# A hybrid decoder trunk: the delta-net stage with TensorE's work in program order, its head parts woven at set distances, and convolutions in thirds

## The chip, the cores and the metric

One core of a Trainium2 chip runs the whole program once. The metric is the device time of that core in microseconds (us), the median of several runs. TensorE multiplies matrices (PE in the profile, PEld its weight loads), VectorE (DVE), ScalarE (ACT) and GpSimd (POOL) work element by element, SyncE (SP) issues most DMAs. Each engine works through its own instructions in a fixed order, and waits on the others by semaphores.

## The reference

A sequence of 1,024 tokens and 16 learned meta tokens (T = 1,040 rows of 1,024) goes through one block with three branches: gated delta-net attention (8 heads of 128), Mamba-2 SSD, and sliding-window attention. They are merged, projected, and followed by an MLP. The change lies in the first branch:

```python
qkv = jax.nn.silu(causal_dwconv(jnp.concatenate([q, k, v], axis=-1), conv_w))   # 4 taps
q, k = l2norm(q), l2norm(k)
beta = jax.nn.sigmoid(b)
g = -jnp.exp(a_log) * jax.nn.softplus(a + dt_bias)          # log decay
...
decay = jnp.exp(jnp.where(tri_incl, gam[..., :, None] - gam[..., None, :], -jnp.inf))
a_low = jnp.where(tri_strict, einsum("bhncd,bhnsd->bhncs", kb, k) * decay, 0.0)
sol = triangular_solve(a_low + eye, rhs, left_side=True, lower=True, unit_diagonal=True)
...
def step(s_state, inp):                                     # over chunks, in order
    v_new = u_c - w_c @ s_state
    o_c = qd_c @ s_state + a_c @ v_new
    s_state = s_state * exp(gl_c) + kt_c.T @ v_new
...
o = rmsnorm(o, norm_w) * jax.nn.silu(gate)
```

## The kernel before

All products are float32 or float32 split in two parts: an operand is a high part (h) plus a low rest (l), and a projection is three products (high by high, high by low, low by high) over 8 blocks of 128 input rows: 24 matmuls for each chunk of columns. The normed input lies in SBUF as `hnh` and `hnl`; the weight's rest is computed by GpSimd (`split_w`, line 118).

A convolution (`conv_steps`, line 342) is a projection over chunks of 348, 346 and 346 columns, 72 matmuls; ScalarE copies each chunk out (`raw`), and when all three are there VectorE does one multiply and three multiply-adds over all 1,040 columns (line 358), then the silu in two halves by a tanh on ScalarE (line 360) and one VectorE step (line 361). A gate (`gdn_gate`, named gg) is a projection over two chunks of 512.

For each head, `gdn_kr` (line 399 on) transposes k (ktp), takes its norms, builds the decay masks dm and the decayed factor qt from rows fetched by DMA (gm), and forms the 128x128 blocks w of the system from k times k (kk; kk0 for the 32 rows of the meta chunk). `gdn_solve` (line 494) inverts the diagonal blocks of 32: it sends them through DRAM into one layout for all (lbd to lb), does 31 pairs of VectorE steps xt and ub (lines 513 and 515), sends the result back through DRAM (ubd to w), and transposes three blocks on VectorE (tt, line 527). `gdn_vr` transposes and scales v (vtp, vt), `gdn_qr` forms q times k (kq, then dm by VectorE, line 478), transposes q for its norms (qtp) and multiplies qt by q on GpSimd (line 469).

What then follows for the head before is its tail. `gdn_levels` (line 532) composes blocks of 32 to 64 and 128 by small matmuls lq, lu, lt, each with a copy by ScalarE. `gdn_scan` (line 576) runs over nine chunks: ks (k times state S), rr on VectorE (line 590), py (line 596), its copy y on ScalarE (line 598), psn (line 603), the new S on VectorE (line 608), and the outputs po. Each step waits for the one before. `gdn_final` normalises: f (VectorE, then a power on GpSimd), vt times f, transposes yf, product with the gate.

The order of the work: `stage_gdn` (line 643) writes head by head: v convolution, final of the head before the last, kr, gate of the last head (with its tail woven in), solve, vr, q convolution, k convolution of the next head, the rest of the tail, qr. Weaving is a generator: a tail yields a number of columns (`WL, WR, WY, WS = 1800, 3200, 2000, 2200`), and each matmul of a projection takes its width off that number (`tick`); at zero the tail makes its next step. So steps of the tail stand between matmuls of a projection. But this order is only written: a scheduler then orders the instructions of each engine by its own estimate of when each is ready, and by priority. Small products outside the weave, such as kk and ktp, are placed by it.

The numbers that follow the names in the listings (`k_3534`) are buffers. "Chain 3" is the levels and the scan of head 3. Heads are counted from 0; the k and v convolutions of head 0 run before the stage, beside the projection smm of the small inputs (b, a, dt), whose transposes (smt), cumulative sums (smg) and rows (smr) make the decays.

## Time and profile before

| | us |
|---|---|
| median of three runs | 2673.28 (2671.59 to 2673.66) |
| profiled execution, its own time | 2672.7 |
| its span | 2670.7 |
| TensorE busy in the span | 2540.5 |
| VectorE busy | 1606.1 |
| ScalarE busy | 1034.6 |
| GpSimd busy | 621.5 |
| mean granted clock of TensorE | 0.979 of full |

The delta-net stage takes from about 78 to 726 us, the SSD stage follows to about 1,140, then sliding window, merge, output projection and MLP. A row of the timeline has start, duration, engine, line, operation, output and inputs, and a count where several of one kind follow each other; in brackets how long the engine had idled and for whom. A row of the waits has the waiting instruction, the one waited for, the total, how often, and the longest. A row of the groups has total busy time and the mean in ns. "Granted clock" is the share of full speed that TensorE was given.

### The profile page before, as it was taken

What the parts mean: (1) busy time and instruction counts of PE and PEld (TensorE: products, weight loads), DVE (VectorE), ACT (ScalarE), POOL (GpSimd) and SP (SyncE); (2) the same over time, 40 slices, a digit from 0 to 9 for tenths busy, and PEclk for the clock granted to TensorE, in tenths of its full rate; (3) what the DMA queues carried; (4) which work ended last, traced back from release to release, by engine and by line L of the source; (5) the groups of instructions that cost most, each with busy time, mean ns of one, the idle gap of its engine ahead of it and who ended that gap; (6) DMA issues with size and microseconds to landing.
All of it is one profiled execution on the core that took longest, in us unless ns stands there. A gap on an engine that the chain in (4) does not pass through costs nothing.

```text
span 2670.7 us, 37466 instructions
## 1 busy us (share of the span) xinstructions
PE 2540.5 (95%) x13983; PEld 2171.0 (81%) x13983; DVE 1606.1 (60%) x3039; ACT 1034.6 (39%) x2581; POOL 621.5 (23%) x491
## 2 busy tenths in 40 slices
PE   6999899999999999999999999999999999999998
PEld 5888788888889989878887888888877788878886
DVE  5776677667557656567673012232426877686878
ACT  4334344334423313355553122121246454444443
POOL 3222222222223323321221222222241000041230
PEclk9989899999999999999999999999999999999999
DMA  3211111111111122231213122131334544566422
GB/s 116 74 37 54 53 53 53 46 48 45 60 63 56 64 72 71 61 83 49 69 52 119 48 67 91 48 111 48 114 122 153 194 169 151 206 243 201 143 87 98
DMA packets 123124, 246.65 MB, mean 92 GB/s; under 512 B 39766, under 2 KB 40182, under 8 KB 122942
## 3 DMA queue, kind: packets, MB, share of 16 engines
q1 hardware_dynamic: 117390, 231.76, 25.9%
q0 software_dynamic: 4544, 11.14, 1.7%
q8 instruction: 110, 1.80, 0.3%
q10 hardware_dynamic: 1008, 1.34, 0.1%
q14 instruction: 72, 0.59, 0.1%
HBM read 183.76 MB, written 54.01 MB: 89 GB/s over the span
## 4 chain that ended last, share of the span: by engine, by line
PE 72%; DVE 18%; issue 3%; DMA 3%; ACT 2%; POOL 2%; SPq 0%; DVEq 0%; POOLq 0%; ACTq 0%
PE dn L1409 10%; PE mgm L149 10%; PE pr L1064 9%; PE up L1214 8%; PE pso L1116 3%; PE x L149 3%; PE gg L149 2%; PE aq L149 2%; DVE xt L513 2%; PE q L149 2%; PE z L149 2%; PE v L149 2%; PE b L149 2%; DVE ub L515 2%; PE c L149 2%
## 5 line engine op out<-in xcount | busy, mean ns | idle before, releaser
L1409 PE MATMUL dn<-wh,ah 128*128 128x512 f32 x448 | 175.4, 391 | 4.3 <-ACT wh L1154 4.3
L1409 PE MATMUL dn<-wl,ah 128*128 128x512 f32 x448 | 175.7, 392 | 0.9 <-POOL wl L1155 0.9
L1409 PE MATMUL dn<-wh,al 128*128 128x512 f32 x448 | 175.5, 392 | 0.0
L1064 PE MATMUL pr<-yl,wph 128*128 128x512 f32 x384 | 150.3, 391 | 1.9 <-DVE yl L137 1.9
L1064 PE MATMUL pr<-yh,wph 128*128 128x512 f32 x384 | 150.2, 391 | 1.9 <-ACT wph L123 1.0
L1064 PE MATMUL pr<-yh,wpl 128*128 128x512 f32 x384 | 149.5, 389 | 0.0
L1074 DVE SCALAR_TENSOR_TENSOR gt<-gt,pr 128x512 f32<-128x512 f32 x32 | 21.9, 687 | 197.5 <-PE pr L1064 197.5
L1155 DVE TENSOR_TENSOR al<-ar,ah 128x512 fp32r<-128x512 f32 x112 | 98.7, 884 | 43.1 <-ACT ah L1154 42.8
L1155 POOL TENSOR_TENSOR wl<-wd,wh 128x512 fp32r<-128x512 f32 x48 | 71.9, 1503 | 194.2 <-ACT wh L1154 63.6
L125 POOL TENSOR_TENSOR wpl<-wpr,wph 128x1024 fp32r<-128x1024 f32 x24 | 61.2, 2549 | 228.0 <-ACT wph L123 217.4
L1154 ACT ACTIVATE ah<-ar 128x512 fp32r<-128x512 f32 x112 | 70.3, 628 | 108.5 <-PE dn L1409 82.8
L123 ACT ACTIVATE wph<-wpr 128x1024 fp32r<-128x1024 f32 x24 | 25.5, 1061 | 210.8 <-PE pr L1064 184.1
L1409 PEld LDWEIGHTS dn<-wh,ah 128*128 128x128 f32 x448 | 84.8, 189 | 22.6 <-ACT wh L1154 4.8
L1409 PEld LDWEIGHTS dn<-wl,ah 128*128 128x128 f32 x448 | 84.8, 189 | 18.9 <-POOL wl L1155 1.2
L149 PE MATMUL mgm<-hnh,mgl 128*128 128x512 f32 x384 | 99.5, 396 | 0.0
L149 PE MATMUL mgm<-hnh,mgh 128*128 128x512 f32 x384 | 99.3, 396 | 0.0
L1409 PEld LDWEIGHTS dn<-wh,al 128*128 128x128 f32 x448 | 84.8, 189 | 17.5
L149 PE MATMUL mgm<-hnl,mgh 128*128 128x512 f32 x384 | 99.0, 396 | 0.0
L125 POOL TENSOR_TENSOR mgl<-mgr,mgh 128x1024 fp32r<-128x1024 f32 x24 | 57.6, 2401 | 164.6 <-PE mgm L149 149.1
L1064 PEld LDWEIGHTS pr<-yl,wph 128*128 128x128 f32 x384 | 72.1, 188 | 19.3 <-DVE yl L137 4.5
L1064 PEld LDWEIGHTS pr<-yh,wph 128*128 128x128 f32 x384 | 72.1, 188 | 19.3 <-ACT yh L136 2.8
L149 PEld LDWEIGHTS mgm<-hnh,mgh 128*128 128x128 f32 x384 | 71.8, 188 | 16.3
(479 smaller groups left out, 7075.6 us busy)
## 6 DMA issues: line engine op xcount, KB each, us to landing
ar<-acd SPq DMA_DIRECT2D x106, 256.0 KB
wu<-in_wup SPq DMA_DIRECT2D x37, 512.0 KB
acd<-s SPq DMA_DIRECT2D x64, 256.0 KB
mgr<-in_win SPq DMA_DIRECT2D x24, 512.0 KB
wpr<-in_wpr SPq DMA_DIRECT2D x24, 512.0 KB
yr<-yd SPq DMA_DIRECT2D x48, 256.0 KB
acd<-c SPq DMA_DIRECT2D x48, 256.0 KB
dms<-rowd SPq DMA_DIRECT2D x16, 512.0 KB
```

Of the source, the lines that this page charges most:

```text
L123: nc.scalar.activation(wh, wr, AF.Copy)
L125: nc.gpsimd.tensor_tensor(wl, wr, wh.bitcast(F32), op=ALU.subtract)
L149: nc.tensor.matmul(ps[:, 0:n], a[:, k, :], b[k][:, c0:c0 + n], start=(i == 0 and k == 0), stop=(i == 2 and k == KT - 1))
L513: nc.vector.tensor_tensor(tv, lb[:, j:j + 1, j + 1:32].broadcast_to([3 * n_, n, m]), ub[:, 0:n, j:j + 1].broadcast_to([3 * n_, n, m]), op= ...
L515: nc.vector.tensor_tensor(ub[:, 0:n, j + 1:32], ub[:, 0:n, j + 1:32], tv, op=ALU.add)
L1064: nc.tensor.matmul(ps, x[:, k, :], y, start=(k == 0 and j == 0), stop=(k == KT - 1 and j == 2))
L1074: nc.vector.scalar_tensor_tensor(t, t, 1.0, ps, op0=ALU.add, op1=ALU.mult)
L1116: nc.tensor.matmul(ps, x[k, th][:, ts], y, start=(k == 0 and j == 0), stop=(k == KT - 1 and j == 2))
L1154: nc.scalar.activation(hi, src, AF.Copy)
L1155: (eng or nc.vector).tensor_tensor(lo, src, hi.bitcast(F32), op=ALU.subtract)
L1214: self.nc.tensor.matmul(ps, x[:, k * P:(k + 1) * P], ops[k][y], start=(j == 0 and k == 0), stop=(j == 2 and k == 3))
L1409: nc.tensor.matmul(acc[t], x[:, t * P:(t + 1) * P], y, start=(i == 0 and m == 0), stop=(i == n - 1 and m == 2))
```

## The change

- During the delta-net stage every matmul and transpose keeps its place in the written order on TensorE (`pin`, `keep_in_program_order`). The other engines' instructions are still placed by the scheduler.
- Several generators run at once, each with its own remaining distance and a scale for it. Not only the tail is woven, but also kr, vr, qr and final, with distances of their own; the tail of head 0 starts 41,000 columns after it is entered, with its distances times 0.55, the others at 7,000, the last at 24,000 with 0.55.
- Convolutions of the stage run in thirds (`conv_pieces`): ScalarE copies a chunk out twice, once scaled by the last tap, VectorE does three multiply-adds, the silu follows for that chunk.
- GpSimd's weight rest and qt times q are four instructions each instead of one. Its product kt times ktc goes; ScalarE scales py by ktc instead (ys), beside the copy y.
- rr, S, w, dm, vt, the transposes tt, the copies of levels, y, ys and po have high priority. The tt transposes are the first step of the tail, no longer the last of the solve; the solve is called at the end of kr.
- At the end of the stage the b and c convolutions of the SSD stage's first group are issued in `stage_gdn`, with the last tail still woven in, and then the last final.

The diff, cut to its core:

```diff
-WL, WR, WY, WS = 1800, 3200, 2000, 2200
+WL, WR, WY, WS = 1800, 3800, 2400, 2900
+RK, RW, RQ = 1500, 3000, 4500
...
-        nc.gpsimd.tensor_tensor(wl, wr, wh.bitcast(F32), op=ALU.subtract)
+        n = 2 if self.pin else KT
+        for k in range(0, KT, n):
+            nc.gpsimd.tensor_tensor(wl[:, k:k + n, :], wr[:, k:k + n, :], wh[:, k:k + n, :].bitcast(F32), op=ALU.subtract)
...
+    def mm(self, *a, **k):
+        i = self.nc.tensor.matmul(*a, **k)
+        return self.tc.keep_in_program_order(i) if self.pin else i
...
     def tick(self, n):
...
+        for co in list(self.cos):
+            co[1] -= n
+            if co[1] <= 0:
+                self.step(co)
...
+    def conv_pieces(self, wt, tag, wcol, name):
...
+        for c0, n, ps in self.proj(wt, CH_ALL, name):
+            d = dst[:, c0:c0 + n]
+            nc.scalar.activation(raw[:, 3 + c0:3 + c0 + n], ps, AF.Copy)
+            nc.scalar.activation(d, ps, AF.Copy, scale=w(3))
+            for j in range(3):
+                nc.vector.scalar_tensor_tensor(d, raw[:, c0 + j:c0 + j + n], w(j), d, op0=ALU.mult, op1=ALU.add)
+            th = self.bt("th", name + "th", [P, 528])[:, 0:n]
+            nc.scalar.activation(th, d, AF.Tanh, scale=0.5)
+            nc.vector.scalar_tensor_tensor(d, th, 1.0, d, op0=ALU.add, op1=ALU.mult)
+            yield
...
-        nc.gpsimd.tensor_tensor(kt, kt, ktc.unsqueeze(2).broadcast_to([P, NC, P]), op=ALU.mult)
-        st.update(qt=qt, dm=dm, w=w, w0=w0, kt=kt, vsc=vsc, bk=bk)
+        st.update(w=w, w0=w0, kt=kt, vsc=vsc, bk=bk, ktc=ktc)
+        self.gdn_solve(st)
...
-            nc.scalar.copy(y[0:n], ps[0:n, 0:P])
+            ys = self.sm.tile([P, P], F32, name="ys", bufs=1)
+            with self.tc.high_priority():
+                if c < NC - 1:
+                    nc.scalar.activation(ys[0:n], ps[0:n, 0:P], AF.Copy, scale=s["ktc"][0:n, c:c + 1])
+                if c > 0:
+                    nc.scalar.copy(y[0:n], ps[0:n, 0:P])
...
     def stage_gdn(self, cur):
         prev = old = None
+        self.pin = True
         for h in range(GH):
...
+                if old:
+                    self.weave(self.gdn_final(old))
+                self.weave(self.gdn_kr(cur), 14000)
+                tail = self.weave(self.gdn_tail(prev), 41000 if h == 1 else 7000, 0.55 if h == 1 else 1.0)
+                self.gdn_v(cur)
+                self.weave(self.gdn_vr(cur), 14000)
+                self.gdn_gate(prev)
+            self.gdn_q(cur)
+            self.weave(self.gdn_qr(cur), 14000)
+            nxt = self.gdn_k(h + 1) if h < GH - 1 else None
             if prev:
+                self.drain(tail)
             old, prev, cur = prev, cur, nxt
+        self.weave(self.gdn_final(old))
+        tail = self.weave(self.gdn_tail(prev), 24000, 0.55)
         self.gdn_gate(prev)
+        self.pin = False
+        st = dict(g=0)
+        self.ssd_b(st)
+        self.ssd_c(st)
         self.drain()
...
     def gdn_tail(self, s):
+        self.gdn_trans(s)
+        yield 4000
         yield from self.gdn_levels(s)
```

Three places show what moves. The first is TensorE at the start of the stage, where smt, smg and smr make the decays of all heads and q is the convolution of head 0. Before:

```order
L256 MATMUL smt<-ident,su 128x32 x6
L149 MATMUL q<-hnh,qh 128x348 x2
L256 MATMUL smt<-ident,su 128x32 x3
L149 MATMUL q<-hnh,qh 128x348 x6
...
L149 MATMUL q<-hnh,ql 128x346 x6
L292 MATMUL smg<-val,tri 128x288
L303 MATMUL smr<-tri,val 32x128 x9
```

Now:

```order
L162 MATMUL smt<-ident,su 128x32 x9
L158 MATMUL smg<-val,tri 128x288
L158 MATMUL smr<-tri,val 32x128 x9
L158 MATMUL q<-hnh,qh 128x348
L162 MATMUL ktp<-ident,k_323 128x128 x4
L158 MATMUL q<-hnh,qh 128x348 x5
```

All of q's matmuls stand behind smg and smr now; 68 of its 72 stood between the last smt and smg before.

The second is where the levels of chain 0 begin on TensorE. Before, they were in the v convolution of head 2, behind the q convolution of head 1 and the k convolution of head 2:

```order
L475 MATMUL kq<-q_1653,k_1025 128x128 x8
L149 MATMUL v<-hnh,vh 128x348 x4
L485 MATMUL qtp<-ident,q_1653 128x128 x4
L149 MATMUL v<-hnh,vh 128x348 x4
L149 MATMUL v<-hnl,vh 128x348 x3
L544 MATMUL lq<-tt,w 32x32 x8
```

Now they are in the gate of head 0, ahead of the q convolution of head 1:

```order
L162 MATMUL vtp<-ident,v_1180 128x128
L158 MATMUL gg<-hnh,ggh 128x512
L158 MATMUL gg<-hnl,ggh 128x512 x2
...
L158 MATMUL gg<-hnl,ggh 128x512 x3
L158 MATMUL lq<-tt,w 32x32 x16
L158 MATMUL gg<-hnl,ggh 128x512 x2
L158 MATMUL lu<-w,qs 32x32 x16
L158 MATMUL gg<-hnl,ggh 128x512
L158 MATMUL gg<-hnh,ggl 128x512
L158 MATMUL lt<-qs,w 32x32 x8
```

They moved ahead by two convolutions, and stand one or two gate matmuls apart.

The third is VectorE at the end of the solve in one of the middle heads. Before (ub ends the solve; k is the convolution of the next head):

```order
L515 TENSOR_TENSOR ub<-ub,xt 99x11
L590 SCALAR_TENSOR_TENSOR rr<-ks,neg,vt 128x128
L608 SCALAR_TENSOR_TENSOR S<-S,egl,psn 128x128
L590 SCALAR_TENSOR_TENSOR rr<-ks,neg,vt 128x128
L353 TENSOR_SCALAR k_3534<-kraw,cols 128x1040
L358 SCALAR_TENSOR_TENSOR k_3534<-kraw,cols,k_3534 128x1040
L478 SCALAR_TENSOR_TENSOR dm<-kq,bk,dm 128x128
L358 SCALAR_TENSOR_TENSOR k_3534<-kraw,cols,k_3534 128x1040
L527 STREAM_TRANSPOSE tt<-w 32x8x32 x2
```

Now:

```order
L574 TENSOR_TENSOR ub<-ub,xt 99x11
L681 SCALAR_TENSOR_TENSOR S<-S,egl,psn 128x128
L657 SCALAR_TENSOR_TENSOR rr<-ks,neg,vt 128x128
L535 SCALAR_TENSOR_TENSOR dm<-kq,bk,dm 128x128 x8
L681 SCALAR_TENSOR_TENSOR S<-S,egl,psn 128x128
L590 STREAM_TRANSPOSE tt<-w 32x8x32 x3
L657 SCALAR_TENSOR_TENSOR rr<-ks,neg,vt 128x128
L394 SCALAR_TENSOR_TENSOR k_4662<-kraw,cols,k_4662 128x348
```

The last rr of the scan stands behind the tt transposes now, all eight dm ahead of them, and the steps of the k convolution behind both.

278 lines of the change are left out of this document (159 added, 119 removed).

## The prediction

> **What bounds the kernel now.** I read the page's slices first, then the busy time by stretch, then the waits of TensorE, and last the timeline at each long wait. The slices say which engine to follow:
>
> ```profile
> PE   6999899999999999999999999999999999999998
> PEclk9989899999999999999999999999999999999999
> ```
>
> TensorE is at nine tenths or more nearly everywhere; past the start and ahead of the last slice the only eights, slice 5 of its busy row and slices 3 and 5 of its granted clock (66.8 us a slice), lie in the delta-net stage (about 78 to 726 us), the only stage whose order the change touches. The busy time by stretch (us; TensorE, its loads, VectorE, ScalarE, GpSimd; clock; DMA), cut where the convolutions of v of heads 3, 4 and 7 and the first one of the next stage begin:
>
> ```profile
> core 0: us, PE busy (x) PEld busy (x) DVE busy (x) ACT busy (x) POOL busy (x), PEclk, DMA share, GB/s
> 77.90:279.40 201.50, 184.39 (x1260) 166.13 (x1259) 143.74 (x354) 81.52 (x265) 54.33 (x38) 0.94 0.19 54
> 279.40:364.00 84.60, 78.78 (x528) 70.65 (x527) 57.61 (x157) 32.91 (x109) 21.26 (x15) 0.88 0.17 45
> 364.00:598.90 234.90, 216.25 (x1580) 195.99 (x1579) 165.56 (x397) 98.70 (x326) 60.16 (x44) 0.99 0.18 53
> 598.90:726.40 127.50, 118.37 (x868) 103.55 (x867) 76.20 (x177) 54.28 (x189) 28.37 (x22) 0.97 0.16 53
> ```
>
> TensorE idles 648.5 - 597.8 = 50.7 us in the stage, and part of its busy time runs at a low clock. The third row is three even heads, 78.3 us each with 6.2 idle. What it waits for (total, times, longest):
>
> ```profile
> PE py L596 <- DVE rr L590: 20.7, 10, 2.6
> PE qtp L485 <- DVE dm L478: 11.8, 6, 2.9
> PE yf L638 <- DVE vt L632: 5.2, 3, 2.2
> PE lq L544 <- DVE tt L527: 3.3, 2, 3.1
> PE kk L445 <- DVE w L442: 3.2, 1, 3.2
> ```
>
> All are waits for VectorE, an engine that is busy two thirds of the time: small steps of the scan (rr) and of the masks (dm) stand in its queue behind convolution steps and blocked ones. The sizes, from VectorE's groups in one solve (total, mean ns, idle before):
>
> ```profile
> L358 DVE SCALAR_TENSOR_TENSOR q<-qraw,cols,q 128x1040 f32<-128x1040 f32 x3 | 3.9, 1292 | 0.0
> L590 DVE SCALAR_TENSOR_TENSOR rr<-ks,neg,vt 128x128 f32<-128x128 f32 x5 | 1.7, 344 | 0.5 <-PE ks L588 0.5
> ```
> Two blocks, from the timelines of VectorE and GpSimd (start, duration):
>
> ```profile
> 496.96 0.24 DVE L513 TENSOR_TENSOR xt<-lb,ub 99x77 f32<-99x77 f32 x1
> 497.64 2.37 DVE L513 TENSOR_TENSOR xt<-lb,ub 99x80 f32<-99x80 f32 x1
> 507.96 2.22 DVE L513 TENSOR_TENSOR xt<-lb,ub 99x40 f32<-99x40 f32 x1
> ...
> 497.53 2.39 POOL L125 TENSOR_TENSOR vl<-vr,vh 128x1024 fp32r<-128x1024 f32 x1 [14.17 <-ACT sqo L617]
> ...
> 507.75 2.37 POOL L469 TENSOR_TENSOR qt<-qt,q 128x1024 f32<-128x1024 f32 x1 [1.70 <-DVE q L361]
> ```
>
> A multiply of 0.24 us takes 2.37 when a whole-tile GpSimd operation began just ahead of it, and ends with it. The low clock has its places too:
>
> ```profile
> 304.86 0.69 PE L544 MATMUL lq<-tt,w 32*32 32x32 f32 x16 [3.08 <-DVE tt L527]
> ...
> 182.00:188.00 6.00, 6.00 (x36) 4.98 (x35) 1.30 (x6) 2.48 (x9) 0.00 (x0) 0.50 0.01 3
> 188.00:194.00 6.00, 6.00 (x23) 5.40 (x22) 2.23 (x9) 0.73 (x2) 0.00 (x0) 0.50 0.00 0
> ...
> 309.00:317.00 8.00, 8.00 (x52) 5.88 (x52) 0.00 (x0) 1.34 (x4) 0.00 (x0) 0.50 0.25 64
> ```
>
> After the levels of chains 0 and 2, TensorE is busy without a gap at half clock for 12 us and more; half of 12 is 6 us lost each time.
>
> **The change, part by part.** The profiled execution spans 2670.7 us and took 2672.7 itself, 0.6 under the median of 2673.28; I sum against 2672.7. About 0.2%, 5.3 us, is what a measurement of this kernel can tell from no change. TensorE's work is the same in kind and number, so only its waits, its clock and the end of the stage count.
>
> Stretch one, 77.9 to 279.4, has two edits that cost. First, q of head 0 no longer stands between the small transposes (smt) and the cumulative sums (smg); VectorE's chain for the gates lies between them:
>
> ```profile
> 77.99 0.46 DVE L264 TENSOR_TENSOR v<-smt,par 128x288 f32<-128x288 f32 x1 [0.79 <-PE smt L256]
> ...
> 80.27 1.95 DVE L272 RECIPROCAL den<-den 128x288 f32<-128x288 f32 x1
> ...
> 83.59 3.91 DVE L280 SCALAR_TENSOR_TENSOR p<-p,s 128x288 f32<-128x288 f32 x8
> ...
> 88.52 0.46 DVE L288 TENSOR_TENSOR val<-spl,fac 128x288 f32<-128x288 f32 x1
> ```
>
> From 77.9 to 89.0 TensorE has nothing: +11.1 us. The cover was q, and nothing else is placed there. At half clock afterwards I add 1.7.
>
> Second, the levels of chain 0 stand before q of head 1, inside the gate of head 0; before, they came two convolutions later. Will their data be there? The first v convolution started at 107.98:
>
> ```profile
> 107.98 1.44 PE L149 MATMUL v<-hnh,vh 128*128 128x348 f32 x8
> ...
> L513 DVE TENSOR_TENSOR xt<-lb,ub 99x84 f32<-99x84 f32 (+23 forms) x31 | 11.1, 357 | 0.8
> L515 DVE TENSOR_TENSOR ub<-ub,xt 99x84 f32<-99x84 f32 (+23 forms) x31 | 6.9, 224 | 0.9
> ...
> 295.47 0.18 DVE L515 TENSOR_TENSOR ub<-ub,xt 99x11 f32<-99x11 f32 x1
> ...
> 304.38 0.43 DVE L527 STREAM_TRANSPOSE tt<-w 32x256 f32<-32x256 f32 x1 [0.49 <-DMA w<-ubd]
> ```
>
> It now starts 12.8 us later, and 3.6 more for the transposes and products placed ahead of it: 124.4. A third of the convolution and its first steps lie before the solve of head 0: about 129.7. The two groups of 31 are a solve of an even head (484.2 to 511.9); xt's mean holds the two blocks, so I take ub's: 62 steps at 0.224 us are 13.9 us; with the other VectorE work that the new order puts between them (nine convolution steps, w, vt, one gate half: some 11 us) and a block or two it ends near 155.5. The round through memory from the last step to the first transpose is 304.38 - 295.65 = 8.7: data at 164. TensorE is there at 124.4 + 11.4 (convolution) + 3.1 + 8.6 (37 gate matmuls) + 1.0 = 148.5. So it waits 16 us (8 if VectorE's order gives way, 21 if GpSimd still blocks it). These levels are close together again, as at 304.86 and longer after a wait; the clock costs between 1.7 and 7, and I take 4.
>
> The Trainium skill's page "TensorE: Matmul & The Clock Gate", Part 1, says that an idle window of some 3.4 us halves the clock and some 3.4 us of work restores it. By that this wait would cost 1.7 us of clock and the sum would be 2.3 lower; the 12 us at 0.50 with TensorE busy don't agree with so quick a return.
>
> What goes in this stretch: its busy time at the even heads' clock is 184.39 x 0.94 / 0.98 = 176.9, and the 17.1 us of waits. What is left per head I take as 2.5 us: rr, S, dm and the copies now go first in VectorE's and ScalarE's queues, and a convolution step is a third as long (1.29 to 0.43), so rr's 2.6 and dm's 2.9 should fall under 1; but the transposes tt now stand ahead of the last chunk's rr, and wait for the 8.7 us round of the solve. Between the solve's end and tt VectorE's new order has only one chunk's steps and eight dm, some 5 us of TensorE's time by the chunk rows below; so rr waits 4 us where the solve ends as late as its place, 0 where it ends early: I take 2. The copies that ScalarE has more of, beside other work, add 0.5. Stretch one: 176.9 + 11.1 + 1.7 + 16 + 4 + 2 x 2.5 = 214.7, against 201.5: +13.2.
>
> Stretch two had a low clock and two stalls: 78.78 x 0.88 / 0.98 = 70.7, and 2.5: 73.2 against 84.6: -11.4. Stretch three: 216.25 + 3 x 2.5 = 223.75 against 234.9: -11.15.
>
> Stretch four: the last chunks of chain 6 are run off before the last gate with nothing between them. What a chunk then takes shows in its three steps of before:
>
> ```profile
> 194.69 0.38 PE L588 MATMUL ks<-S,k 128*128 128x128 f32 x2
> ...
> 195.54 0.47 PE L596 MATMUL py<-rr,w 128*128 128x128 f32 x2
> ...
> 196.42 0.49 PE L603 MATMUL psn<-y,kt 128*128 128x128 f32 x2
> ...
> 197.35 0.49 PE L588 MATMUL ks<-S,k 128*128 128x128 f32 x2
> ```
>
> A chunk is 2.66 us from ks to ks, about 1.1 of it its own matmuls; three without cover lose near 5 us, and 2 for the clock. With 3 more for the yf transposes and the levels of chain 7 (yf waited 5.2 in all before) it is 118.4 + 10 = 128.4 against 127.5: +0.9. (0 to 7 more if the levels of chain 7, dense at a scale of 0.55, halve the clock.)
>
> The rest costs nothing or little. GpSimd loses kt times ktc and ScalarE gains eight copies and the scaled convolution copies, three for each of three convolutions a head:
>
> ```profile
> L598 ACT COPY y<-py 128x128 f32<-128x128 f32 (+1 forms) x9 | 2.4, 263 | 12.7 <-PE py L596 12.6
> L349 ACT ACTIVATE kraw<-k 128x346 f32<-128x346 f32 (+1 forms) x3 | 1.4, 461 | 5.0 <-PE k L149 5.0
> ...
> 442.20:519.80 77.60, 71.05 (x529) 64.37 (x528) 55.01 (x133) 32.90 (x109) 19.91 (x15) 1.00 0.18 53
> ```
>
> 8 x 0.26 + 9 x 0.46 = 6.2, so ScalarE goes from 32.9 busy of 77.6 to about 39, beside TensorE; were its cover gone, a copy of a level would be 1 to 3 us late. Quarters cut the longest block from 2.4 to 0.6. The first b and c convolutions only moved in the code. Sum: 13.2 - 11.4 - 11.15 + 0.9 = -8.5; 2672.7 - 8.5 = 2664.2 us.
>
> **The rivals.**
>
> *Faster still: the start hides itself, and the even heads get near their floor.* If solve 0 is done when its levels come (less of VectorE's other work before it), 16 + 4 go; if a head keeps 1.5 us of waits, six heads give 6 more: 2664 - 26 = 2638. For it: the rr waits have causes that the change removes. Against it: the reckoning of 164 against 148.5.
>
> *Slower: the last chunk waits for tt in every head.* If the solve isn't shortened by the quarters, its data come 4 us late or more: rr of the last chunk stands behind tt in VectorE's queue, py behind rr, po and the following k matmuls behind py. At 7 us a head instead of 2.5 the six heads give back 27: 2691. It decides from 2.5 + 8.5 / 6 = 3.9 us a head upwards; from 4.8 it is slower by more than the bound. For it: before, tt stood after that rr; twelve quarters now start about a solve, and each can catch a step for up to 0.6 (a quarter of 2.4), 7.2 us in all where the blocks of 497.64 and 507.96 cost 4.1 over a free step. The page "SBUF — State Buffer" of the Trainium skill, section "Who interferes with whom", has a VectorE instruction with two SBUF inputs and a GpSimd one that reads SBUF hold the shared pair for the whole instruction, whoever is first; by that rule the quarters shorten the longest block and not their total, which the two blocks above agree with and no run here shows for quarters. Against it: VectorE is free for 77.6 - 55.0 = 22.6 us of an even head, so a late solve can catch up.
>
> *The change does nothing on balance*: the start costs 28 and the even heads bring 28, so 2673, within 5.
>
> **How the numbers follow.** My forecast 0.32 (0.26 of it faster by over 0.2%, 0.06 within). The faster rival 0.26, the slower 0.28, no balance 0.14 (0.08 within, 0.06 slower). Faster 0.52, same 0.14, slower 0.34. The likeliest case alone runs from 2652 (wait of 8, clock of 1.7) to 2676 (wait of 21, clock of 7). Together the range goes from 2628, somewhat under the faster rival, to 2692, the slower one.
>
> **What would show it.** Right: the smg wait of 11 us near 78 to 89 and a wait for tt of 8 to 21 us ahead of the first lq; the v convolution of head 3 starting later than 279.4 by 10 to 16, and then heads of 73 to 75 us; rr and dm waits of under 1 us; no xt step over 1 us. Wrong: q filling the time to smg; levels of chain 0 without a wait; heads of 78 us or more with py waiting for the last rr, which would be the slower rival; heads of 71, the faster one. The stages after the delta net should keep their length.

## The result and the profile after

| | before | after |
|---|---|---|
| median, us | 2672.44 (2668.52 to 2673.66, 4 runs) | 2718.61 (2716.36 to 2719.69, 4 runs) |
| profiled span, us | 2670.7 | 2718.0 |

The ratio is 1.0174 [1.0157, 1.0192]: the kernel got slower by 46 us; faster was forecast, and the time lies above the predicted range of 2628 to 2692. The slices of the page say at once that the loss isn't spread evenly (TensorE's busy tenths and its granted clock, 68 us a slice):

```profile
PE   6679889888999999999999999999999999999998
PEclk8879999999999999999999999999999999999999
```

The stage lies in slices 2 to 12 (77.9 to 768.6 us). Cut at the same instructions as in the prediction (v convolutions of heads 3, 4 and 7, first x convolution), and with that x convolution as a fifth row:

```profile
77.90:309.60 231.70, 187.59 (x1263) 168.91 (x1264) 147.74 (x429) 94.91 (x312) 54.17 (x72) 0.87 0.16 46
309.60:391.70 82.10, 72.78 (x529) 65.81 (x528) 55.71 (x152) 38.52 (x129) 21.76 (x29) 0.98 0.17 50
391.70:637.60 245.90, 218.02 (x1581) 197.19 (x1580) 166.87 (x451) 115.34 (x382) 64.78 (x85) 0.98 0.17 50
637.60:768.60 131.00, 117.58 (x846) 103.28 (x846) 71.89 (x178) 57.74 (x193) 28.06 (x32) 0.95 0.14 43
768.60:799.40 30.80, 28.42 (x188) 27.21 (x187) 21.20 (x20) 12.62 (x31) 8.37 (x6) 1.00 0.20 69
```

| stretch | before | after | difference | forecast |
|---|---|---|---|---|
| one, to v of head 3 | 201.5 | 231.7 | +30.2 | +13.2 |
| two, head 3 to 4 | 84.6 | 82.1 | -2.5 | -11.4 |
| three, heads 4 to 7 | 234.9 | 245.9 | +11.0 | -11.15 |
| four, to x | 127.5 | 131.0 | +3.5 | +0.9 |
| x convolution on | the rest | the rest | +5 | 0 |

The sum is +47, as the spans say. Every middle head now takes 82.0 us (473.7 to 555.7 and its neighbours), where 74 was forecast. The waits of TensorE (total, times, longest), over the stage:

```profile
PE yf L162 <- DVE vt L707: 24.4, 7, 4.2
PE ks L158 <- DVE S L681: 15.9, 12, 2.8
PE lq L158 <- DVE tt L590: 13.5, 2, 12.4
PE smg L158 <- DVE val L304: 11.2, 1, 11.2
PE vtp L162 <- DVE vt L510: 10.3, 1, 10.3
PE py L158 <- DVE rr L657: 7.2, 10, 1.2
PE lq L158 <- ACT qs L608: 4.0, 6, 1.7
```

The waits for rr and dm have shrunk as forecast: py waits 7.2 in all instead of 20.7, and the 11.8 of qtp are gone. But the list is longer than before at the top. Three waits belong to the start (smg, vtp, lq for tt); yf and ks recur in every head.

**The start.** The wait of smg is the forecast one, 11.2. That of vtp (transposes of v of head 0) was overlooked. The timeline of ScalarE, GpSimd and VectorE shows its chain:

```profile
95.69 0.27 ACT L457 COPY kt<-ktp 128x128 f32<-128x128 f32 x1 [0.32 <-PE ktp L162]
...
99.06 1.05 ACT L439 ACTIVATE qt<-gm 128x1024 f32<-128x1024 f32 x1
...
101.64 0.29 ACT L460 ACTIVATE jk<-kt 128x128 f32<-128x128 f32 x1
...
106.97 1.80 POOL L473 TENSOR_TENSOR vsc<-vs,ppos 128x9 f32<-128x9 f32 x1 [1.95 <-DVE vs L471]
...
108.81 1.55 DVE L510 TENSOR_TENSOR vt<-vtp,vsc 128x512 f32<-128x512 f32 x3 [1.74 <-POOL vsc L473]
...
109.55 0.47 PE L162 MATMUL vtp<-ident,v 128*128 128x128 f32 x1 [10.32 <-DVE vt L510]
```

The norms of k (jk) could begin at 95.7, when the last kt is copied, but ScalarE takes them from 101.6 on, in turn with the exponentials of dm, which wait for the rows gm by DMA. From the norms come the factors vsc, from them vt, and two groups of four transposes fill the buffers; the ninth transpose, first of the third group, waits for the first vt, and the rest of the q convolution waits behind it, in order. Then the first lq of chain 0 in TensorE's timeline:

```profile
173.72 1.06 PE L158 MATMUL lq<-tt,w 32*32 32x32 f32 x16 [12.41 <-DVE tt L590]
```

and the slices of 8 us behind it (columns as in the prediction: five busy times, clock, DMA):

```profile
174.00:182.00 8.00, 6.51 (x75) 4.84 (x73) 7.06 (x28) 2.15 (x5) 0.00 (x0) 0.50 0.01 2
182.00:190.00 8.00, 8.00 (x51) 6.20 (x50) 1.78 (x8) 1.89 (x4) 0.00 (x0) 0.50 0.00 1
190.00:198.00 8.00, 8.00 (x45) 6.65 (x45) 6.39 (x23) 2.76 (x9) 2.79 (x4) 0.87 0.24 66
```

A wait of 12.4 (16 was forecast), and half clock until about 192, 18 us after work began again. Some 17 us of that were busy, so 8 to 9 us were lost (4 was forecast).

**A middle head.** 82.0 us hold 72.7 busy and 9.3 idle, of which 4.1 are yf's wait and 2.3 those of ks. In the timelines of VectorE, ScalarE, GpSimd and TensorE the chain of yf reads (the last row is a group of VectorE over the head, with total and mean):

```profile
472.25 0.98 ACT L392 ACTIVATE k<-k,cols 128x348 f32<-128x348 f32 x2
...
472.57 3.65 POOL L128 TENSOR_TENSOR ggl<-ggr,ggh 128x256 fp32r<-128x256 f32 x4 [4.66 <-PE k L158]
...
472.89 6.01 DVE L394 SCALAR_TENSOR_TENSOR k<-kraw,cols,k 128x348 f32<-128x348 f32 x7 [0.87 <-ACT k L392]
...
478.82 0.15 DVE L704 SCALAR_TENSOR_TENSOR f<-ms,qe 128x8 f32<-128x8 f32 x1
...
481.04 1.23 DVE L707 TENSOR_TENSOR vt<-vt,f 128x1024 f32<-128x1024 f32 x1 [0.17 <-POOL f L706]
...
482.32 1.11 PE L162 MATMUL yf<-ident,vt 128*128 128x128 f32 x4 [4.14 <-DVE vt L707]
...
L394 DVE SCALAR_TENSOR_TENSOR q<-qraw,cols,q 128x346 f32<-128x346 f32 (+1 forms) x9 | 5.1, 570 | 0.0
```

The last ks of the scan (471.25) is the last reader of one of two k buffers, and the first step of the new k convolution writes into it: ScalarE's scaled copy. Though its raw copy was made at 459.2, the scaled one comes at 472.25. All of k's steps then land together on VectorE. Seven of them take 6.01 us: the first five 0.78 to 1.41 each, beside GpSimd's work, the other two 0.57, which is also what a step of q takes (570 ns in the mean). The final's f stands behind all seven, and yf, held in its place, waits. So a step of a third takes 0.57, and not the 0.43 (a third of 1.29) of the prediction. What makes ks wait for S in every head was not tried apart.

### The profile page after: what moved, and what is told of

Same layout as the page of the kernel before. It is cut to its first block, busy times and chain, and to the rows that moved or that the text cites. A ratio compares the mean times of both kernels' runs of the same rounds, so it can differ in the third digit from the quotient of the medians.

```text
span 2718.0 us, 37896 instructions
## 1 busy us (share of the span) xinstructions
PE 2539.1 (93%) x13983; PEld 2169.6 (80%) x13983; DVE 1612.6 (59%) x3171; ACT 1077.9 (40%) x2725; POOL 635.8 (23%) x597
## 4 chain that ended last, share of the span: by engine, by line
PE 70%; DVE 18%; ACT 4%; issue 3%; DMA 2%; POOL 2%; SPq 0%; DVEq 0%; ACTq 0%; POOLq 0%
PE dn L158 10%; PE mgm L158 9%; PE pr L158 9%; PE up L158 9%; PE gg L158 3%; PE pso L158 3%; PE aq L158 3%; PE pv L158 2%; PE x L158 2%; DVE ub L574 2%; DVE xt L572 2%; PE z L158 2%; PE c L158 2%; PE b L158 2%; PE v L158 1%
## 5 line engine op out<-in xcount | busy, mean ns | idle before, releaser
L128 POOL TENSOR_TENSOR mgl<-mgr,mgh 128x1024 fp32r<-128x1024 f32 x24 | 57.6, 2400 | 167.0 <-PE mgm L158 150.8
```

The costliest lines, as they stand in the source:

```text
L128: nc.gpsimd.tensor_tensor(wl[:, k:k + n, :], wr[:, k:k + n, :], wh[:, k:k + n, :].bitcast(F32), op=ALU.subtract)
```

## The experiments

The theory at the outset: with the order held, each wait of TensorE adds to the time, so taking away the cause of one shortens every head by it. The rivals: the clock, or another engine's queue, takes it back; or the quarters on GpSimd cost more than they bring. A head is the distance from one v convolution's first matmul to the next.

| kernel | edit | v of head 3 at | middle heads | x at | median us |
|---|---|---|---|---|---|
| before | | 279.4 | 77.6 to 84.7 | 726.4 | 2672.4 |
| after | | 309.6 | 82.0 | 768.6 | 2718.6 |
| e1 | final later | | 81.9 | | 2724.2 |
| e2 | order free | 288.7 | 82.0 to 84.9 | | 2700.3 |
| e5 | third k buffer | 307.2 | 81.3 to 82.8 | 765.7 | 2720.6 |
| e7 | whole convolutions | 313.1 | 85.4 to 86.3 | 790.5 | 2740.0 |
| e9 | scan ends earlier | 309.5 | 76.0 to 83.8 | 753.9 | 2705.8 |
| e17 | halves apart | 309.0 | 82.0 to 89.7 | 786.1 | 2736.5 |
| e13 | halves apart, scan earlier | 308.6 | 73.9 | 730.3 | 2687.9 |
| e19 | e13, head 0 free | 308.6 | 73.9 | 726.8 | 2680.1 |
| e14 | e13, order free | 288.2 | 73.9 | 703.0 | 2658.8 |
| e18 | e14, third k buffer | 285.5 | 73.8 to 74.6 | 699.7 | 2654.5 |

### Does taking a wait away shorten a head?

First the final is moved back, behind VectorE's burst of k steps:

```diff
 def gdn_final(self, s):
-        yield 8000
+        yield 19500
```

> The changed kernel with one number changed: the transposes yf of the final come 19,500 columns after the final's first step, not 8,000. Nothing else. Theory 1 (waits at the woven places add up: yf's wait is a wait of its own, because f stands behind seven convolution steps and a power on GpSimd, and v's first chunk of 24 matmuls is all that covers it): the yf waits, 24.4 us in seven places, go to under 4, the even head falls from 82.0 to 78.0 +- 0.7 us and the kernel by 20 to 25 us, to about 2695. Theory 2 (the heads are bound by a chain through VectorE and ScalarE, and TensorE's waits only move): the levels, kk or the scan wait instead, the head stays at 81 us or more and the kernel at 2713 or more.

2724.24 us, ratio to before 1.0201 [1.0136, 1.0266]. yf's wait fell from 24.4 to 1.2 us in all, and the heads stayed at 81.9. The longest wait but those of the start, then one head and a slice of 4 us in a later one:

```profile
PE lq L158 <- ACT qs L608: 17.6, 6, 4.4
```

```profile
394.10:476.00 81.90, 74.99 (x528) 67.37 (x528) 55.48 (x151) 38.58 (x128) 21.76 (x29) 0.94 0.17 50
...
570.00:574.00 4.00, 3.55 (x38) 3.10 (x38) 0.28 (x1) 0.95 (x3) 0.00 (x0) 0.50 0.00 0
```

The levels, now without yf's wait ahead of them, come into the burst: the second half of lq waits for a copy in ScalarE's queue, and the clock halves. Against the changed kernel's head, idle time fell from 9.3 to 6.9, and busy time rose from 72.7 to 75.0. The theory that waits add up falls. Next the cause itself goes: a third buffer for k (paid for by one buffer of the tanh, and by a constant that is loaded by DMA instead of copied by GpSimd).

```diff
-        self.tags = dict(raw=2, th=3, qv=1, gm=1, k2=2, kt=3, vt=2, dm=2, w=2, gt=1, qt=2)
-        self.xtags = dict(lb=1, ub=1, xt=1, qs=1, x4=2, hs=3, vb=2)
+        self.tags = dict(raw=2, th=2, qv=1, gm=1, k2=2, kt=3, vt=2, dm=2, w=2, gt=1, qt=2)
+        self.xtags = dict(k2b=1, lb=1, ub=1, xt=1, qs=1, x4=2, hs=3, vb=2)
...
-        return dict(h=h, k2=self.together(self.gdn_in(h, 1, "k2", "k"))[0])
+        return dict(h=h, k2=self.together(self.gdn_in(h, 1, "k2b" if h % 3 == 2 else "k2", "k"))[0])
```

> The changed kernel with a third buffer for the convolved k (the tanh pieces have two buffers instead of three for it, and the identity of the solve is loaded by a DMA instead of copied by GpSimd, to make room). Theory 3: a third of the k convolution writes its scaled copy straight into the destination, and that buffer is still read by ks of the chain two heads back until its last chunk; so ScalarE's scaled copies stand until 472.25 though the first raw copy is there at 459.23, and all nine VectorE steps of k burst into the next head. With a third buffer the steps of two thirds of k come ahead of tt, VectorE's 5 us of idle time there are used, and the even head falls from 82.0 to 75 to 78 us, the kernel by 25 to 40 us to 2680 to 2695. Theory 2b (the head is bound by the sum of VectorE's work with its blocks, not by this buffer): heads of 81 us or more, the kernel over 2710.

2720.55 us, ratio 1.0198 [1.0116, 1.028]. yf's wait halved (11.7 in all, none over 1.8), so the buffer was a cause of it; heads 81.3 to 82.8 with 73.9 to 75.5 busy at clocks of 0.94 to 0.96. Both edits together:

> The same with yf 19,500 columns after the final's first step, as in the first experiment, where it gained nothing. Theory 3: there ScalarE's queue stood behind the tanh of k, which waited for the burst, and the wait moved from yf to lq; with the burst gone the later yf gains what is left of its wait: 0 to 2 us a head below the third buffer alone, and lq waits for qs under 1 us each. Theory 2b: as there, heads of 81 us or more.

2728.71 us, ratio 1.0229, heads of 82.4 to 86.9 and lq waiting 21.1 us for qs. The wait was removed or halved in three ways, and the median rose by 2 to 10 us: what a head gains in waits it loses in clock. The next edit ends the tail earlier, all its distances shortened:

```diff
-    tail = self.weave(self.gdn_tail(prev), 41000 if h == 1 else 7000, 0.55 if h == 1 else 1.0)
+    tail = self.weave(self.gdn_tail(prev), 41000 if h == 1 else 7000, 0.55 if h == 1 else 0.8)
```

> The changed kernel with the distances of every middle tail at 0.8: the last ks of a chain comes some 7 us earlier in the k convolution, and so the buffer of k is free earlier; no buffer is added. Theory 3: the burst of k's steps starts earlier by as much, yf's wait of 4.1 us falls under 1, the head to 77 to 79 us, the kernel to 2690 to 2705. Theory 2b: chunks at 0.8 run into their own chain (rr, S, ys waits grow by 3 us a head or more) and the head stays at 81 us or more.

2705.84 us, ratio 1.0143 [1.0075, 1.0211], and the most telling run. yf waits 3.6 us in all. The middle heads have the same order and nearly the same idle time (4.4 to 4.8), yet take 83.5, 76.0, 79.1 and 83.8. Two of them by engine, and five slices in the last:

```profile
309.50:393.00 83.50, 79.01 (x527) 70.95 (x527) 55.05 (x151) 39.27 (x130) 21.47 (x28) 0.90 0.17 49
393.00:469.00 76.00, 71.57 (x529) 64.28 (x528) 54.84 (x151) 38.82 (x127) 21.35 (x28) 1.00 0.19 54
...
560.00:564.00 4.00, 4.00 (x28) 3.54 (x28) 0.00 (x0) 1.34 (x5) 0.00 (x0) 0.50 0.02 4
564.00:568.00 4.00, 4.00 (x25) 3.49 (x24) 0.00 (x0) 1.29 (x5) 0.00 (x0) 0.50 0.00 0
568.00:572.00 4.00, 4.00 (x24) 3.48 (x24) 1.74 (x3) 2.33 (x8) 0.00 (x0) 0.50 0.00 0
572.00:576.00 4.00, 4.00 (x18) 4.00 (x17) 1.70 (x9) 2.41 (x13) 1.03 (x1) 0.51 0.00 0
576.00:580.00 4.00, 4.00 (x26) 3.33 (x26) 1.84 (x8) 1.42 (x2) 0.78 (x1) 1.00 0.00 0
```

and TensorE's levels just ahead of those slices and in them:

```profile
555.60 0.69 PE L158 MATMUL lq<-tt,w 32*32 32x32 f32 x16 [0.45 <-ACT qs L608]
...
557.21 0.69 PE L158 MATMUL lu<-w,qs 32*32 32x32 f32 x16
558.70 0.95 PE L158 MATMUL lu<-w,qs 32*32 32x32 f32 x16 [0.80 <-ACT w L617]
...
569.60 1.97 PE L158 MATMUL lu<-w,qs 64*64 64x64 f32 x16
```

The two heads differ by 7.5 us, and 7.4 of it is busy time (79.01 against 71.57) at another clock. In the last head, as slow as the first, TensorE works without a gap for 16 us at half speed, after two waits in the levels, 0.45 ahead of the second lq and 0.80 ahead of the second lu. The earlier scan brings a head's idle time from 9.3 to 4.4 (76.0 - 71.57); the clock then decides. In the changed kernel itself the clock behaves otherwise:

```profile
482.00:486.00 4.00, 3.68 (x16) 3.62 (x17) 2.73 (x7) 1.78 (x7) 0.31 (x1) 0.57 0.01 3
486.00:490.00 4.00, 3.47 (x57) 2.77 (x55) 1.53 (x3) 1.27 (x4) 0.00 (x0) 1.00 0.32 131
```

There the wait of yf takes it to 0.57 from 482 to 486, and from 486 on, all through the levels, it is 1.00. "TensorE: Matmul & The Clock Gate" of the Trainium skill, Part 1, has the clock halve after an idle window of about 3.4 us and come back after as much work. yf's 4.14 us of idling and 4 us of return agree with that; 16 us at half clock, fully busy, after waits under 1 us don't.

The clock records of the traces, from which the clock column is reckoned, say more. Between 60 and 800 us every stretch of one clock is a whole number of steps of 3.41 us long. In e9 the half clock ends with the first step that holds no small matmul (572.5 to 576.0; the last small one, lu, starts at 569.60), and in the changed kernel the one step at half clock behind yf (482.2 to 485.7) holds none either. It is so in most places. In 19 traces (all but e4's), from 130 us to 800, a step at half clock in which TensorE was busy for 97% or more was followed by full clock in 87 of 97 cases where it held no matmul of 32x32 or 64x64, and by half clock again in 167 of 190 where it held ten or more. What sets the half clock off is another matter: of the steps at full clock with ten or more small matmuls, 353 of 359 were followed by full clock where TensorE was busy for nine tenths or more, and 35 of 45 by half clock where it was busy for less than eight tenths (10 of 44 between). Without small matmuls half a step's work was enough: full clock followed in 2,664 of 2,665 cases. So waits among small matmuls set it off, and small matmuls alone, without a wait, keep it on. This is counted, not tried by an experiment of its own.

It also bears on why a wait taken away changed nothing. The middle heads last 24 such steps (81.9 us) in the changed kernel, in e1 and, but for the first, in e17, with one, three and two of them at half clock, and 25 steps (85.3) in e3 and, again but for the first, in e7. Whether a head that loses the clock once in each round falls into the steps' rhythm was not tried.

### Which part of the change does what?

The order left to the scheduler, everything else as in the changed kernel:

```diff
     def mm(self, *a, **k):
         i = self.nc.tensor.matmul(*a, **k)
-        return self.tc.keep_in_program_order(i) if self.pin else i
+        return i
```

> The changed kernel, all of it, but matmuls and transposes of the stage are no longer held in program order on TensorE: the scheduler may place them, as before the change. Its order then has q of head 0 between smt and smg again, the levels of chain 0 in the k convolution of head 2 and yf some twelve matmuls later. Theory 1 (the held order is what costs: it demands data at places where VectorE has not got to yet): waits at smg, vtp and the first lq, 35 us together, fall under 8; the kernel comes to 2670 to 2685. Theory 2 (thirds, quarters and more ScalarE work lengthen the chains whatever the order is): 2700 or more, with even heads of 80 us or more. Between them both have a part.

2700.33 us, ratio 1.0111 [1.005, 1.0173]: 18 less. v of head 3 begins at 288.7 instead of 309.6; the waits of smg and of lq for tt are gone, that of vtp is 15.8. The heads are no better (82.0 to 84.9, clock 0.88 to 0.92). So the held order costs about 21 us at the start. GpSimd's work whole again:

```diff
-        n = 2 if self.pin else KT
+        n = KT
```

> The changed kernel with GpSimd's weight rest and qt times q in one instruction each again, not in four. Theory A (a quarter holds the port as long as the whole does, and four in a row block four steps of VectorE one after the other): time within 5 us of the changed kernel, 2713 to 2723; the group of convolution steps on k, now 865 ns in the mean where a free one takes some 430, stays over 700. Theory B (quarters do shorten the blocks): slower by 5 to 15 us, ks and rr waits over 2 us come back. Theory C (quarters cost more than they save): faster by 5 us or more.

2751.82 us, ratio 1.0304 [1.024, 1.0368]: 33 more, over twice what theory B allowed, with heads of 85.2. One of GpSimd's groups over the middle heads, in the changed kernel:

```profile
L128 POOL TENSOR_TENSOR vl<-vr,vh 128x256 fp32r<-128x256 f32 x12 | 8.5, 735 | 0.0
```

in this one, with its waits of TensorE over the stage:

```profile
L128 POOL TENSOR_TENSOR vl<-vr,vh 128x1024 fp32r<-128x1024 f32 x3 | 7.4, 2451 | 42.2 <-ACT y L669 42.2
```

```profile
PE ks L158 <- DVE S L680: 19.0, 13, 2.0
...
PE py L158 <- DVE rr L656: 11.1, 10, 1.5
```

Four quarters take 2.94 us where the whole takes 2.45, and still win: the waits for S and rr are longer with whole operations (15.9 and 7.2 with quarters). A head has 10.9 idle instead of 9.3 (85.2 - 74.3), and 1.6 more of clock. The page "SBUF — State Buffer" of the Trainium skill, "Who interferes with whom", makes the ports that the two engines share an exclusive lock. The prediction took from it that quarters shorten the longest block and not the total. The first part agrees with the runs (a step of k takes 2.43 us at most with whole operations, 1.41 with quarters); of the total something goes too, since VectorE's busy time of a head is 57.6 with whole operations and 55.6 with quarters. Together it is worth 33 us. The rival that quarters cost more than they bring falls. Convolutions whole again (the changed kernel with the line in `conv_steps` that branches to `conv_pieces` taken out):

```diff
-        if self.pin:
-            return (yield from self.conv_pieces(wt, tag, wcol, name))
```

> The changed kernel with whole-length convolutions as before the change (one multiply and three multiply-adds over 1,040 columns, two halves of tanh), all else kept: order, weaving, quarters, ScalarE's ys. Theory 3 (a third gains nothing while the destination isn't free, and costs ScalarE a scaled copy and VectorE nothing less): about the same as the changed kernel, 2705 to 2730, yf and rr waiting behind steps of 1.3 us. A rival (the thirds themselves are the loss): under 2690. The other rival (thirds do shorten the blocks for rr and S): 2735 or more.

2740.01 us, ratio 1.0271: 21 more, heads of 85.4 to 86.3. The thirds help too, but not in the way the rival says: a head of e7 has 6.9 idle (85.5 - 78.6), less than the 9.3 with thirds, ks and py wait 10.0 and 5.5 in all (15.9 and 7.2 with thirds), and what it loses is clock, 0.90 against 0.98. The tail of head 0 later:

```diff
-    tail = self.weave(self.gdn_tail(prev), 41000 if h == 1 else 7000, 0.55 if h == 1 else 1.0)
+    tail = self.weave(self.gdn_tail(prev), 55000 if h == 1 else 7000, 0.45 if h == 1 else 1.0)
```

> The changed kernel with the tail of head 0 entered after 55,000 columns, not 41,000, and its distances at 0.45, not 0.55: its levels come in the third part of the q convolution's first chunk, some 6.4 us of matmuls later. Theory 1 (waits add up): the wait for tt at the first lq falls from 12.4 to about 6, the kernel by 4 to 7 us. Theory 2 (the tail then runs into its own chain, 2.66 us a chunk, and loses it again): the kernel within 3 us of before this edit, with waits of rr, S and y in the q and k convolutions of head 1 and 2 grown by 4 us or more.

Inconclusive: the two runs, 2726.32 and 2768.39, lie too far apart, and the trace is of the longer one. In it the wait of lq for tt is 8.5 instead of 12.4.

### What keeps the clock?

In the held order the two halves of lq stand back to back, and so do those of lu, the second half behind ScalarE's copy of the first. The distances can be changed, or the halves separated. Levels far apart:

```diff
-WL, WR, WY, WS = 1800, 3800, 2400, 2900
+WL, WR, WY, WS = 3600, 3040, 1920, 2320
```

(and 0.65 for the two scales of 0.55, as in all kernels below but the one with the halves alone, which keeps 0.55)

> The changed kernel with the scan's distances at 0.8 as in the run before, and the distance between the levels doubled, 1,800 to 3,600 columns (the two short tails at 0.65). Theory 4 (the levels, small matmuls of 32x32 and 64x64 close behind one another, pull the granted clock down to 0.50 for 12 to 16 us, 6 to 8 us a head, whenever the waits that stood ahead of them go; that is why a wait taken away gives nothing back): with some eleven convolution matmuls between two levels in place of six, the heads run at a clock of 0.98 or more and take 75 to 77 us each, and the kernel comes to 2680 to 2690. Rival (the clock falls whatever is between the levels, or for another cause): heads between 76 and 84 us as in the run before, clock 0.90 to 1.00, kernel 2700 to 2715.

2732.64 us, ratio 1.0254, heads of 81 to 88; yf waits 21.0, py 15.9. Wider distances alone don't do it; they bring the waits back as well, so this run doesn't test the distance by itself. The same with the order free:

> The same distances with TensorE's order free, as in the second experiment, whose start was 21 us shorter and whose heads ran at a clock of 0.92. Theory 4: the start keeps its gain and the heads come to 75 to 78 us: 2660 to 2675, about the kernel before. Rival (a free order packs the levels together again, the written distances don't matter): heads of 80 us or more at a clock of 0.92, kernel 2690 or more.

2692.18 us (2675.67 to 2704.37), ratio 1.0092, heads of 77.5 to 85.6 at clocks of 0.88 to 1.00. The levels packed (WL 900):

> The opposite: the scan's distances at 0.8 and the distance between the levels halved, 900 columns. Theory 4: the clock falls in every head, heads of 82 us or more at 0.90 or less, kernel 2705 to 2730. Rival (distance does not matter): heads between 76 and 84 us as at 1,800, kernel near 2706; or shorter stretches of half clock since the small matmuls are over sooner: under 2700.

2734.63 us, ratio 1.0259, clocks of 0.90 to 0.92. Then matmuls of the convolution between the two halves, with WL 2400 and the scan as short as in the spread:

```diff
-WL, WR, WY, WS = 1800, 3800, 2400, 2900
+WL, WR, WY, WS = 2400, 3040, 1920, 2320
...
                 nc.scalar.copy(q[hi:hi + 32, :, 0:32], v(ps, hi, hi + 32, 32))
-        yield WL
+            yield WL // 2
...
                 nc.scalar.copy(u[lo:hi, :, hi:hi + 32], v(ps, lo, hi, 32))
-        yield WL
+            yield WL // 2
```

> The run with the scan's distances at 0.8, its level distance at 2,400, and one more place to weave at: between the two halves of lq and of lu, which stand back to back in program order, the second behind ScalarE's copy of the first (0.45 to 0.8 us each). Before the change kk and gate matmuls stood between the halves and the clock stayed at 1.00 there. Theory 4b (the clock falls where the small matmuls stand with those short waits between them, not where they are merely near one another): no waits of lq and lu for ScalarE, clock 0.98 or more in every middle head, heads of 74 to 77 us, kernel 2680 to 2692. Theory 2b (the loop through VectorE sets the head): heads of 80 us or more, whatever the clock, with the waits at yf, rr or S.

2687.88 us, ratio 1.007 [1.0045, 1.0095]. Each middle head takes 73.9, the forecast 74 of the prediction. One head by engine, and TensorE at the first level of another:

```profile
382.50:456.40 73.90, 71.47 (x528) 64.02 (x527) 55.12 (x151) 38.63 (x129) 20.98 (x28) 1.00 0.19 56
```

```profile
463.04 0.69 PE L158 MATMUL lq<-tt,w 32*32 32x32 f32 x16
463.65 0.89 PE L158 MATMUL v<-hnl,vh 128*128 128x346 f32 x4
464.47 0.69 PE L158 MATMUL lq<-tt,w 32*32 32x32 f32 x16
```

Busy 71.47 at clock 1.00 and 2.4 idle; no wait stands in the levels. The halves alone, without the earlier end of the scan and with WL 1800:

> The changed kernel with one edit: the two halves of lq and of lu stand half a distance apart (convolution matmuls between them); the scan ends where the change puts it (scale 1.0, WL 1800). Theory: the halves hold the clock and the earlier end of the scan takes away the waits of yf and ks, two separate things. Then the clock of the middle heads is 0.98 to 1.00 and the waits of yf (about 4 us a head) and ks (about 2) stay: heads of 79 to 81, total 2695 to 2712. Rival A: the halves alone do all, heads of 74 to 75.5, total 2680 to 2692. Rival B: the halves do nothing without the earlier scan, heads of 81.5 to 83.5, clock under 0.96 in some of them, total 2712 to 2725.

2736.54 us, ratio 1.0235 [1.0203, 1.0267]: heads of 82.0 (the first 89.7), the case of rival B in the heads and above even its total, since the first middle head and the end of the stage got longer too. yf's wait is back, 23.2 in all, and so is its idle time, 8.4 a head. So neither edit alone brings 73.9: the scan's earlier end takes out the waits (4.4 idle in e9, at a clock that falls in some heads), and the halves, with that, hold the clock and leave 2.4 idle. What WL 2400 instead of 1800 adds wasn't tried apart. Two further distances and the third buffer, on the halves: the tail entered at 22,000 columns, into the gate, with the distances of the scan at 0.65,

> The order held, but the levels of the middle heads in the gate as before the change, among 512-column matmuls (the tail enters after 22,000 columns, not 7,000; the scan's distances at 0.65 to end in the same place). Theory 4b: clock 0.98 or more, and the scan at 0.65 pays rr and S waits of 2 to 4 us a head: heads of 77 to 80 us, kernel 2690 to 2705. Theory 2b: the same waits and yf's, heads of 82 us or more, kernel 2715 or more.

2742.99 us, ratio 1.0271, heads of 79 to 89, py waiting 11.7, yf 12.9 and kk 9.4. Theory 4b fails here: the halves stand apart, lq and lu don't wait for ScalarE, and still the clock is 0.86 to 0.87 in three of the four middle heads (88 to 89 us, 82.0 busy). In the first of them kk waits 1.21 us for w until 336.98, just ahead of lq at 337.58. So the halves apart don't hold the clock by themselves. And the third buffer in place,

> The level halves and the scan at 0.8 with the third buffer for k as well. Theory 3 (the buffer holds back the steps of k) with 4b: one to two us a head below the run without the third buffer. If the buffer no longer matters where the scan ends early: the same within 1 us a head.

2671.52 us, ratio 1.0014 [0.9997, 1.003]: the heads are as without it (73.9), so the buffer has nothing left to bring there; of the profiled runs' 13.7 us 5.5 lie ahead of the x convolution and some 6 in the SSD stage behind it, and why isn't settled.

### The start, and the best version

The order of head 0 alone left to the scheduler, on e13:

```diff
         for h in range(GH):
+            self.held = h > 0
...
-        return self.tc.keep_in_program_order(i) if self.pin else i
+        return self.tc.keep_in_program_order(i) if self.held else i
```

> Halves of the levels apart, scan at a scale of 0.8, the order of TensorE held from head 1 on and left to the scheduler in head 0 alone (decays, k, v and q of head 0, k of head 1). In the same kernel with everything held the v convolution of head 3 begins at 308.6, with nothing held at 288.2. Theory 1: the waits of smg (11.2) and of the third transpose of v (10.3) are what the held order costs at the start, each filled by q's matmuls when the order is free; the v convolution of head 3 then begins at 287 to 294. Rival: the solve of head 0 sets the time of the first lq (its data come at about 186), so what the two waits give back is lost again in front of lq, whose wait grows from 12 to 25 us or more; the v convolution of head 3 then begins at 302 to 308. Heads 73.9 either way; total 2660 to 2675 by theory 1, 2680 to 2690 by the rival.

2680.09 us, ratio 1.003 [1.0013, 1.0046]. v of head 3 begins at 308.64, where it does with everything held (308.59): near the rival's 302 to 308, but not by its mechanism, since lq waits no longer than with everything held. The waits:

```profile
PE vtp L162 <- DVE vt L510: 15.7, 1, 15.7
PE lq L158 <- DVE tt L590: 12.2, 1, 12.2
```

and slices behind the wait, at the levels of chain 1:

```profile
230.00:238.00 8.00, 7.41 (x46) 6.54 (x47) 5.09 (x10) 2.80 (x9) 0.30 (x2) 0.50 0.38 152
238.00:246.00 8.00, 8.00 (x62) 7.00 (x61) 0.52 (x1) 3.69 (x13) 0.00 (x0) 0.50 0.00 0
```

The whole front moved by 8.2 us (v of head 1 at 127.8 instead of 136.0), and the half clock from 230 to 250, where the kernel with everything held has 3.4 us of it, took that back. So freeing head 0 has brought nothing by head 3. What the free order brings it brings behind v of head 1: to v of head 2 it takes 85.2 us in e14 and 94.6 here, where the levels of chain 0 hold up everything behind them, and to v of head 3 another 75.2 and 86.2, with the clock. e14, the halves with the order free throughout:

> The same distances and halves, TensorE's order free. Theory 4b: the free order's shorter start (21 us) and heads of 75 to 78 us give 2660 to 2672. Theory 2b: heads of 80 us, 2685 or more.

2658.78 us, ratio 0.9974 [0.9954, 0.9993], heads of 73.9 and v of head 3 at 288.2: 29 us less than with the order held. And with the third buffer:

> Halves of the levels apart, scan at a scale of 0.8, the order of TensorE left to the scheduler, and a third buffer for k. The third buffer left the heads at 73.9 us where the order was held, and took a few us off the start and the end. Theory: heads of 73.5 to 74.5 again, total 2645 to 2662, under the kernel before by 0.2 to 0.9%. Rival: with the k steps free of their buffer the scheduler orders ScalarE's and VectorE's queues anew, levels wait for qs and the clock falls as in the changed kernel with the third buffer alone: heads of 76 or more in part, total 2665 to 2690.

2654.45 us, ratio 0.993 [0.9904, 0.9957]: the best version, 64 us under the changed kernel and 0.7% under the kernel before. A head in it:

```profile
360.10:433.90 73.80, 71.38 (x527) 63.95 (x526) 55.09 (x151) 38.34 (x129) 20.57 (x27) 1.00 0.19 58
```

## Why the prediction was wrong

- **Stretch one, forecast +13.2, measured +30.2.** The wait for smg was right, 11.1 (measured 11.2). That for tt, 16 (12.4), is near by luck: TensorE came to the first lq at 161.3 and not at 148.5, and its data at 173.7 and not at 164, so both ends were 10 to 13 late. The step that failed first is "3.6 more for the transposes and products placed ahead of it: 124.4": these products had a chain over ScalarE, GpSimd and VectorE behind them that was not followed, and TensorE waited 10.3 for it; v of head 1 began at 134.8. The clock after lq was sized at 4, with 7 as the most; it was 18 us at half speed, so 8 to 9, and all the busy time of the stretch is 5 over the forecast. The waits of yf, ks, kk and the like in the two heads of this stretch came to some 10 where 5 was allowed. So 10.3 for vtp, 5 for the clock and 5 for these waits, less the 3.6 by which tt's wait was shorter, make the 17.
- **Stretches two and three, forecast -11.4 and -11.15, measured -2.5 and +11.0.** The step is "What is left per head I take as 2.5 us". It was sized from rr, S and dm, the waits of before, and those did shrink. It left out that the new order makes other waits: idle time is 9.3 a head. The scaled copy of the k convolution needs its target buffer after the first third, where the old VectorE steps began after the last; the final's steps queue behind the burst. That is yf's 4.1; ks's 2.3 for S were put at nothing too. A convolution step was sized at 0.43 and takes 0.57 where nothing blocks it. The scaled copies were put under "costs nothing or little", with ScalarE's cover as the only price. 9.3 idle instead of 2.5 makes 6.8 of the 8 us that a head is over its forecast; the other 1.2 is clock (72.7 busy against 71.5 at full clock).
- **The clock was treated as a term of the start and the end only.** The even heads were reckoned at 0.98 with no reason why. e1, e5 and e9 show that a head without yf's wait loses time to the clock in its place (2.3 us in e1, 7.4 in the slow heads of e9), and e13 that it needn't. The prediction's 73 to 75 is what e13 has, two edits later.
- **The rivals.** The slower one, the last chunk's rr waiting for tt, was not it: that py waits 0.7 a head. Its size, 2691, was too small too, because it knew only one cause. The faster one's point, the start hiding itself, is refuted by the wait of 12.41 at 173.72, and "nothing on balance" by the 46 us.
- **Stretch four and after, forecast +0.9 and 0, measured +3.5 and +5.** The last chunk of chain 7 and the last final's transposes now lie inside the x convolution, with two waits of 1.2, and x takes 30.8 instead of 25.7: some work only crossed the cut.
- **What was right**: the wait for smg, the wait for tt at the first levels, waits for rr of 1.2 us at most and none for dm (under 1 was the sign), no xt step over 1 us (0.79 at most in the stage, 2.38 before), and that quarters and thirds each bring something (33 and 21 us by e3 and e7, the thirds by way of the clock).
- **A sum of its own.** The likeliest case "from 2652 to 2676" doesn't follow from the values named beside it: 8 and 1.7 for 16 and 4 give 2654, 21 and 7 give 2672. The outcome doesn't turn on it.

## What to carry to other kernels

When an order is held by hand, follow for each instruction that is put early the whole chain that feeds it, on every engine and down to which buffer its first writer needs; the waits that the change removes say nothing on those it makes. Before counting the removal of a wait as a gain, look at the granted clock of a head without it: here it was worth nothing until the small matmuls behind it were also spread among large ones, and spreading them was worth nothing (e17, e15) while other waits stood around them. Time the middle heads singly: two heads with the same order and waits and different lengths are the clock.

## What the runs showed of the hardware

- The clock changes in steps of 3.41 us. Half clock lasted 16 us with TensorE fully busy, after levels of small matmuls (32x32) with waits of 0.45 and 0.80 (e9); it ended with the first step without small matmuls. By the counts over 19 traces, waits among small matmuls set it off and small matmuls alone keep it on. In e13, with four large matmuls between the halves and no wait there, it didn't come.
- A wait of 4.1 us ahead of the levels costs its own time and one step at half clock, 3.41 us, which holds no small matmul in the changed kernel; then the levels ran at full clock. Two waits under 1 us inside the levels cost five steps in two of the middle heads of e9, two steps in a third and none in the fourth. So a long wait ahead of the levels did less harm to the clock than two short ones inside them could.
- Four quarters of a GpSimd operation take 2.94 us against 2.45 for the whole, and the kernel is 33 us faster with them.
- A multiply-add of VectorE over a third of the columns takes 0.57 us where nothing blocks it, and one over all of them 1.29: more than a third.
